# Softmax of 32 attention tiles: division moved into the transposing products, bias added by an identity product

## The chip, the cores and the metric

One NeuronCore of a Trainium2 chip runs the whole program. The metric is device time in microseconds (us), the median of the runs. The core has a matrix engine (PE, with its weight loads shown as PEld), a vector engine (DVE), a scalar engine (ACT), a general engine (POOL) and queues that issue transfers (SP above all). Each engine executes its own instructions in the order in which they stand; engines wait for each other by semaphores. PE reads both operands from SBUF and writes to PSUM banks of 128 x 512 f32.

## The reference: what is computed

Two layers on 256 latent tokens and 256 context tokens of width 1024. The first layer is attention and a dense feed-forward block, the second a pooling mixer and a mixture of eight experts. The change touches the attention's softmax alone:

```
s_loc = q . k * scale + bias         # neighbourhood heads: 8 heads, latent keys, bias and mask by head
s_ctx = q . k_ctx * scale            # the same heads, context keys, no bias
p = softmax(concat(s_loc, s_ctx))    # f32; the latent-attention heads (8 more) have no bias
out = p[:, :n_loc] @ v + p[:, n_loc:] @ v_ctx
```

All tensors are f32, and everything must come out to f32 accuracy.

## The kernel before

Attention works on 32 units. A unit is one head and 128 queries, so its scores are one PSUM bank of 128 queries x 512 keys. A block is a pair of heads with both query halves, four units. Blocks 4 to 7 (units 0 to 15) are the latent-attention heads, with scores from `QT` and `KT` (L605); blocks 0 to 3 (units 16 to 31) are the neighbourhood heads, with scores from `qaT` and `kaT` (L603) and a bias. There are three score banks, called `w`; the six products that build the bias table (L583) use them too.

For each unit `softmax` does: for neighbourhood units an add of the bias into the first 256 columns of the bank (DVE, L616); the negated row maximum (DVE, L618) and, for the latent units, its scaling (L621); exponential with row sums (ACT, L623) into an SBUF tile `sc`, of which there are four; reciprocal of the sums (DVE, L624); and the division of the 128 x 512 tile by a scalar for each row (DVE, L625). `turn` then transposes the tile in four 128 x 128 pieces on PE: L633 calls the helper whose line is L168, with the data as stationary and the identity as moving side, into a bank of `acc`; ACT copies that to `PT` (L633). When a block's four units are turned, `values` multiplies with the values (L641, bank `o`), ACT and DVE split the result in a high and a low part (L154, L155), and `project` multiplies these with a quarter of the output weights in three products each (L159 to L161).

The code runs over units: at every even unit i the scores of units i+4 and i+5 are issued, then unit i is turned, and values and projections follow by block. Three modulation jobs run alongside: eight DVE multiply-adds of 128 x 512 each (L316) and a few PE products (L345). POOL multiplies the output weights by the gate g1, four 128 x 2048 tiles (L650), and takes the low parts of the second half's weights (L155). The order on every engine but SP is set by a list scheduler at build time until the last unit is issued, so the code's order is a wish and not the order executed. After the attention the second half of the projection, the residual with its norm, and the feed-forward block follow on PE.

Of the kernel before, what the change touches and what calls it, by code (L numbers as in the profile page):

```python
# [7 lines left out]
F32 = mybir.dt.float32  # L8
# [3 lines left out]
OP = mybir.AluOpType  # L12
# [5 lines left out]
P = 128  # L18
D = 1024
KB = D // P  # L20
S = 256
# [81 lines left out]
class Trunk:  # L103
# [247 lines left out]
    def layer0_attention(self):  # L351
        tc, nc, I = self.tc, self.nc, self.I
# [3 lines left out]
        with ExitStack() as st:  # L356
            ent = lambda *a, **k: st.enter_context(tc.tile_pool(*a, **k))
            ap = ent(name="attn", bufs=1)
# [138 lines left out]
            qcT = ap.tile([P, 2, S], F32, name="qcT")  # L497
# [43 lines left out]
            qaT = ap.tile([P, 4, S], F32, name="qaT")  # L541
            kaT = ap.tile([P, 4, 512], F32, name="kaT")
            for j in range(4):
                t = self.ps()
# [10 lines left out]
            for j in range(4):  # L555
                t = self.ps()
# [12 lines left out]
            for rr in range(2):  # L569
                for h in range(8):  # L570
                    nc.sync.dma_start(brev[h // 4][rr * 64:rr * 64 + 64, (h % 4) * 384:(h % 4 + 1) * 384].rearrange("p (a b) -> p a b", a=6),
                                      bass.AP(tensor=rb.tensor, offset=rb.offset + h * 465 + (5 - rr) * 31 - 48,
                                              ap=[[1, 64], [31, 6], [1, 64]]))
# [3 lines left out]
            bias = ap.tile([P, 3200], F32, name="lw")[:, 0:3072].rearrange("p (h a b) -> p h a b", h=8, a=6)  # L577
# [12 lines left out]
            w_out = I["attn_w_out"][0].rearrange("(k p) f -> p k f", p=P)  # L590
            blocks = (4, 5, 6, 7, 0, 1, 2, 3)
            units = [(blk, u, qt) for blk in blocks for qt in range(2) for u in range(2)]
            scs, PTs, ws, wp = {}, {}, {}, {}

            def scores(i):

                s_ps = [self.ps() for _ in range(2)]
                for n in range(2):
                    blk, u, qt = units[i + n]
                    h = (blk % 4) * 2 + u  # L600
                    qs = slice(qt * P, (qt + 1) * P)
                    if blk < 4:
                        nc.tensor.matmul(s_ps[n], qaT[u * 64:u * 64 + 64, blk, qs], kaT[u * 64:u * 64 + 64, blk], start=True, stop=True)  # L603
                    else:
                        nc.tensor.matmul(s_ps[n], QT[:, h, qs], KT[:, h], start=True, stop=True)  # L605
                for n in range(2):
                    softmax(i + n, s_ps[n])

            def softmax(i, s_ps):
                blk, u, qt = units[i]  # L610
                h = (blk % 4) * 2 + u
                nmax = self.sm.tile([P, 1], F32, name="nmax", bufs=4)
                sc = tmp.tile([P, 512], F32, name="sc", bufs=4)
                scale = 1.0
                if blk < 4:
                    nc.vector.tensor_add(s_ps[:, 0:S], s_ps[:, 0:S],  # L616
                                         bias[:, h, 2 - 2 * qt:6 - 2 * qt].rearrange("p a b -> p (a b)"))
                nc.vector.reduce_max(nmax, s_ps, axis=AX.X, negate=True)  # L618
                if blk >= 4:
                    scale = MLA_SCALE  # L620
                    nc.vector.tensor_scalar(nmax, nmax, scale, None, op0=OP.mult)  # L621
                den = self.sm.tile([P, 1], F32, name="den", bufs=4)
                nc.scalar.activation(sc, s_ps, AF.Exp, bias=nmax, scale=scale, accum_out=den)  # L623
                nc.vector.reciprocal(den, den)  # L624
                nc.vector.tensor_scalar(sc, sc, den, None, op0=OP.mult)  # L625
                scs[i] = sc

            def turn(i):
                blk, u, qt = units[i]
                if (blk, u) not in PTs:  # L630
                    PTs[blk, u] = tmp.tile([P, 4, S], F32, name="PT", bufs=5)
                self.transposes(PTs[blk, u][:, :, qt * P:(qt + 1) * P], [scs[i][:, kt * P:(kt + 1) * P] for kt in range(4)],
                                lambda d, t: nc.scalar.copy(d, t.rearrange("p (k q) -> p k q", k=4)), self.acc)  # L633

            def values(blk):
                o_ps = self.ps("o")
# [30 lines left out]
            def meanwhile(k2):  # L667
                if k2 in (1, 2):
                    scores(2 * k2 - 2)
                if k2 > 1:  # L670
                    next_mod()
# [7 lines left out]
            for tt in range(4):  # L679
                t = self.acc()  # L680
# [5 lines left out]
            for i, (blk, u, qt) in enumerate(units):  # L686
                if i in (8, 16, 26):
                    self.mod_finish(int(i < 26), "o")
                    if mods:
                        self.mod_issue(*mods.pop(0))  # L690
                if i in (2, 4, 6, 8, 10, 12):
                    bias_block(i // 2 - 1)
                if i % 2 == 0 and i + 4 < len(units):
                    scores(i + 4)
                turn(i)
                if i % 4 == 0 and i:
                    values(units[i - 1][0])
                if i % 4 == 2:
                    if i > 4:
                        project(0, i // 4 - 1)  # L700
                    out_split(0, blk, w0[:, 2 * (i // 4 % 2):2 * (i // 4 % 2) + 2])
                if i == 16:
                    out_stream(1)
                if i == 19:

                    places = [ap.tile([P, 8, 512], F32R, name="t16"), ap.tile([P, 4, 512], F32R, name="o8"), e8k(0, F32R)]
                    later = [t[:, 2 * j:2 * j + 2] for t in places for j in range(t.shape[1] // 2)]
                if i > 20 and later:
                    out_split(1, blocks[8 - len(later)], later.pop(0), nc.gpsimd)
# [3 lines left out]
            for w in self.ffn_first[:2]:  # L713
                t = self.stream_slot().bitcast(F32R).rearrange("p (i k f) -> p i k f", i=2, k=KB)
# [11 lines left out]
            t = self.ps("o")  # L726
# [1009 lines left out]
```

## Time and profile before

| | |
|---|---|
| median of 3 runs | 1456.23 us (1454.86 to 1461.7) |
| profiled execution | 1459.44 us, span 1457.6 us |
| PE busy | 1360.4 us, 93% of the span |
| DVE, ACT, POOL busy | 725.8, 465.0, 105.4 us |
| mean granted TensorE clock | 0.97 |
| attention's units on PE | from 137 to about 237 us of the span |

PE's granted clock has two levels, 2.4 GHz (1.00 in the rows) and 1.2 GHz (0.50). A matmul's record includes the time until its last result is out, and the records of neighbours overlap; so the price of a product in a full stream is the distance between the starts, not the record's length. An f32 product is recorded as two matmuls; a row of the timeline merges neighbours of one kind and gives their count.

### The profile page before, as it was taken

To read this page: it belongs to the slowest core of one execution; us is meant where nothing else is said; L and a number is where in the kernel's file an instruction comes from. 1 tells how busy PE (TensorE), PEld (TensorE's weight loads), DVE (VectorE), ACT (ScalarE), POOL (GpSimd) and SP (SyncE) were. 2 spreads that over 40 slices of the span, in tenths; PEclk is the share of its full clock that TensorE was granted. 3 is DMA by queue.
4 is the path that set the end of the run, shared out by engine and by line. 5 is a ranking of instruction groups with operands and counts; after the bars stand their busy time and mean duration, and the time that the engine had idled before them with its cause. 6 is when DMAs were issued, how large, how long until landed. Compare 5 with 4: busy or idle time off the path is not lost. (4 is left out here: it accounts for less than half of the span.)

```text
span 1457.6 us, 22081 instructions
## 1 busy us (share of the span) xinstructions
PE 1360.4 (93%) x8817; PEld 841.2 (58%) x8817; DVE 725.8 (50%) x1156; ACT 465.0 (32%) x691; POOL 105.4 (7%) x66
## 2 busy tenths in 40 slices
PE   6898989799999999999999999999999999999995
PEld 4765546699998586555664333343333344667762
DVE  2769795587677765754572100011100015556653
ACT  3443462443442343544550000010000013345541
POOL 0344040301001100000000000000000000000000
PEclk9999989799999999999999999999999999999998
DMA  9775422699886669999999999999999999999994
GB/s 361 257 230 191 153 76 68 211 371 326 306 295 185 133 254 392 375 395 393 365 367 380 381 393 393 395 355 368 392 396 393 392 370 361 393 390 393 377 352 168
DMA packets 237561, 464.41 MB, mean 319 GB/s; under 512 B 31655, under 2 KB 76922, under 8 KB 237454
## 3 DMA queue, kind: packets, MB, share of 16 engines
q1 hardware_dynamic: 234582, 457.61, 87.1%
q10 hardware_dynamic: 2872, 5.33, 1.1%
q8 instruction: 71, 1.16, 0.3%
q14 instruction: 36, 0.29, 0.1%
HBM read 461.87 MB, written 1.05 MB: 318 GB/s over the span
## 5 line engine op out<-in xcount | busy, mean ns | idle before, releaser
L155 DVE TENSOR_TENSOR wh<-wt,wh 128x1024 fp32r<-128x1024 f32 (+1 forms) x243 | 291.9, 1217 | 78.8 <-ACT wh L154 71.9
L1649 PE MATMUL w<-wt,xg 128*32 128x256 f32 (+3 forms) x2496 | 314.3, 468 | 16.5 <-DMA wt<-in_moe_w_up_dram 16.5
L154 ACT CAST wh<-wt 128x1024 fp32r<-128x1024 f32 (+1 forms) x244 | 252.1, 1042 | 179.8 <-PE w L160 81.3
L1649 PEld LDWEIGHTS w<-wt,xg 128*32 128x32 f32 (+1 forms) x2496 | 120.7, 122 | 178.0 <-issue 125.5
L1709 PE MATMUL acc<-wt,aT 128*32 128x256 f32 (+2 forms) x1456 | 188.1, 464 | 0.0
L1656 DVE TENSOR_TENSOR a<-a,w 64x512 f32<-64x512 f32 (+4 forms) x58 | 31.2, 538 | 304.8 <-ACT a L1655 304.8
L1655 ACT ACTIVATE a<-w 64x512 f32<-64x512 f32 (+4 forms) x58 | 27.1, 467 | 427.9 <-PE w L1649 426.2
L1709 PEld LDWEIGHTS acc<-wt,aT 128*32 128x32 f32 (+2 forms) x1456 | 67.0, 120 | 105.8 <-issue 87.4
L316 DVE SCALAR_TENSOR_TENSOR raw<-wt,ccol,raw 128x512 f32<-128x512 f32 x105 | 101.2, 965 | 2.1
L161 PE MATMUL acc<-wh,aT 128*128 128x512 f32 x204 | 79.7, 391 | 0.0
L159 PE MATMUL w<-h2H,wh 128*128 128x256 f32 x272 | 77.2, 284 | 0.0
L161 PE MATMUL w<-h2H,wh 128*128 128x256 f32 x272 | 76.2, 280 | 0.0
L160 PE MATMUL w<-hT,wh 128*128 128x256 f32 x272 | 76.2, 280 | 0.0
L1620 POOL TENSOR_TENSOR wt<-wt,ln_g 128x256 f32<-128x256 f32 x1 | 1.0, 1013 | 954.0 <-ACT wt L1618 954.0
L160 PE MATMUL w<-wh,xgH 128*128 128x512 f32 (+1 forms) x144 | 56.6, 393 | 1.6 <-DVE wh L155 1.6
L159 PE MATMUL w<-wh,xgH 128*128 128x512 f32 (+1 forms) x144 | 56.8, 394 | 0.0
L161 PE MATMUL w<-wh,xgL 128*128 128x512 f32 (+1 forms) x144 | 55.7, 387 | 0.0
L160 PEld LDWEIGHTS w<-hT,wh 128*128 128x128 f32 x272 | 51.5, 189 | 0.6 <-issue 0.2
L161 PEld LDWEIGHTS w<-h2H,wh 128*128 128x128 f32 x272 | 51.6, 190 | 0.0
L159 PEld LDWEIGHTS w<-h2H,wh 128*128 128x128 f32 x272 | 51.1, 188 | 0.6 <-issue 0.2
L1649 PE MATMUL o<-wt,xg 128*32 128x256 f32 (+2 forms) x416 | 49.2, 459 | 0.0
L159 PE MATMUL acc<-wh,aH 128*128 128x512 f32 (+1 forms) x112 | 45.3, 404 | 0.0
(499 smaller groups left out, 2075.7 us busy)
## 6 DMA issues: line engine op xcount, KB each, us to landing
wt<-in_moe_w_down_dram SPq DMA_DIRECT2D x104, 1024.0 KB
wt<-in_moe_w_gate_dram SPq DMA_DIRECT2D x96, 1024.0 KB
wt<-in_moe_w_up_dram SPq DMA_DIRECT2D x96, 1024.0 KB
wt<-in_mod_w_dram SPq DMA_DIRECT2D x45, 1024.0 KB
wt<-in_moe_w_gate_dram SPq DMA_DIRECT2D x16, 896.0 KB
wt<-in_moe_w_up_dram SPq DMA_DIRECT2D x16, 896.0 KB
wt<-in_ffn_w_gate_dram SPq DMA_DIRECT2D x11, 1024.0 KB
wt<-in_ffn_w_up_dram SPq DMA_DIRECT2D x11, 1024.0 KB
```

The costliest lines, as they stand in the source:

```text
L154: nc.scalar.copy(hi, src)
L155: return (eng or nc.vector).tensor_sub(lo, src, hi.bitcast(F32))
L159: nc.tensor.matmul(out, lh, rh, start=start, stop=False, skip_group_check=True)
L160: nc.tensor.matmul(out, lh, rl, start=False, stop=False, skip_group_check=True)
L161: return nc.tensor.matmul(out, ll, rh, start=False, stop=stop, skip_group_check=True)
L316: nc.vector.scalar_tensor_tensor(acc, w[k], self.ccol[:, k:k + 1], mb if k == 0 else acc, op0=OP.mult, op1=OP.add)
L1620: eng.tensor_mul(o[:, cs], o[:, cs], g[:, hs][:, cs])
L1649: nc.tensor.matmul(t[b:b + M, 0:f1 - f0], xg[:, k], w[k][:, f0:f1], start=(k == 0), stop=(k == KB - 1), skip_group_check=True)
L1655: nc.scalar.activation(a[64:64 + r, f0:f1], t[0:r, f0:f1], AF.Silu)
L1656: nc.vector.tensor_mul(a[0:r, f0:f1], a[64:64 + r, f0:f1], t[64:64 + r, f0:f1])
L1709: nc.tensor.matmul(dacc[0][q2 * M:(q2 + 1) * M, 0:Dn], aT[0:bw, b, q * M:(q + 1) * M], wd[j][0:bw, q2 * Dn:(q2 + 1) * Dn], start=(first an ...
```

## The change

The division of the whole tile is gone. In its place DVE multiplies the 128 x 128 identity by the reciprocals, a scalar for each row, which gives a diagonal matrix (L639 of the changed kernel; four slots in one tile, named qcT like the tile whose memory it takes). The transposing products take this diagonal as moving side and are written as plain products (L642) instead of transposes. The DVE add of the bias is gone as well. PE adds it: after the scores of a neighbourhood pair, one product for each unit with the identity as stationary side and 256 columns of the bias table as moving side accumulates into the bank (L611). All else is as before.

```diff
--- before.py
+++ after.py
@@ -590,7 +590,8 @@
             w_out = I["attn_w_out"][0].rearrange("(k p) f -> p k f", p=P)
             blocks = (4, 5, 6, 7, 0, 1, 2, 3)
             units = [(blk, u, qt) for blk in blocks for qt in range(2) for u in range(2)]
-            scs, PTs, ws, wp = {}, {}, {}, {}
+            scs, dens, PTs, ws, wp = {}, {}, {}, {}, {}
+            dgs = ap.tile([P, 4, P], F32, name="qcT")
 
             def scores(i):
 
@@ -600,9 +601,16 @@
                     h = (blk % 4) * 2 + u
                     qs = slice(qt * P, (qt + 1) * P)
                     if blk < 4:
-                        nc.tensor.matmul(s_ps[n], qaT[u * 64:u * 64 + 64, blk, qs], kaT[u * 64:u * 64 + 64, blk], start=True, stop=True)
+                        nc.tensor.matmul(s_ps[n], qaT[u * 64:u * 64 + 64, blk, qs], kaT[u * 64:u * 64 + 64, blk], start=True, stop=False,
+                                         skip_group_check=True)
                     else:
                         nc.tensor.matmul(s_ps[n], QT[:, h, qs], KT[:, h], start=True, stop=True)
+                for n in range(2):
+                    blk, u, qt = units[i + n]
+                    if blk < 4:
+                        nc.tensor.matmul(s_ps[n][:, 0:S], self.ident,
+                                         bias[:, (blk % 4) * 2 + u, 2 - 2 * qt:6 - 2 * qt].rearrange("p a b -> p (a b)"),
+                                         start=False, stop=True, skip_group_check=True)
                 for n in range(2):
                     softmax(i + n, s_ps[n])
 
@@ -612,9 +620,6 @@
                 nmax = self.sm.tile([P, 1], F32, name="nmax", bufs=4)
                 sc = tmp.tile([P, 512], F32, name="sc", bufs=4)
                 scale = 1.0
-                if blk < 4:
-                    nc.vector.tensor_add(s_ps[:, 0:S], s_ps[:, 0:S],
-                                         bias[:, h, 2 - 2 * qt:6 - 2 * qt].rearrange("p a b -> p (a b)"))
                 nc.vector.reduce_max(nmax, s_ps, axis=AX.X, negate=True)
                 if blk >= 4:
                     scale = MLA_SCALE
@@ -622,15 +627,21 @@
                 den = self.sm.tile([P, 1], F32, name="den", bufs=4)
                 nc.scalar.activation(sc, s_ps, AF.Exp, bias=nmax, scale=scale, accum_out=den)
                 nc.vector.reciprocal(den, den)
-                nc.vector.tensor_scalar(sc, sc, den, None, op0=OP.mult)
+                dens[i] = den
                 scs[i] = sc
 
             def turn(i):
                 blk, u, qt = units[i]
                 if (blk, u) not in PTs:
                     PTs[blk, u] = tmp.tile([P, 4, S], F32, name="PT", bufs=5)
-                self.transposes(PTs[blk, u][:, :, qt * P:(qt + 1) * P], [scs[i][:, kt * P:(kt + 1) * P] for kt in range(4)],
-                                lambda d, t: nc.scalar.copy(d, t.rearrange("p (k q) -> p k q", k=4)), self.acc)
+
+                dg = dgs[:, i % 4]
+                nc.vector.tensor_scalar(dg, self.ident, dens[i], None, op0=OP.mult)
+                t = self.acc()
+                for kt in range(4):
+                    nc.tensor.matmul(t[:, kt * P:(kt + 1) * P], scs[i][:, kt * P:(kt + 1) * P], dg, start=True, stop=True,
+                                     skip_group_check=True)
+                nc.scalar.copy(PTs[blk, u][:, :, qt * P:(qt + 1) * P], t.rearrange("p (k q) -> p k q", k=4))
 
             def values(blk):
                 o_ps = self.ps("o")
```

On PE, neighbourhood units 20 to 24 and their surroundings, first before, then changed (L603 and L604 are scores, L168 and L642 a unit's turn, L641 and L652 values, L159 to L161 the projection):

```order
L603 MATMUL w<-kaT,qaT 128x512 x2
L168 MATMUL acc<-cst,sc 128x128 x4
L641 MATMUL o<-PT,e_1114 64x256 x8
L168 MATMUL acc<-cst,sc 128x128 x4
L603 MATMUL w<-kaT,qaT 128x512 x2
L168 MATMUL acc<-cst,sc 128x128 x4
```

```order
L604 MATMUL w<-kaT,qaT 128x512 x2
L611 MATMUL w<-lw,cst 128x256 x2
L642 MATMUL acc<-qcT,sc 128x128 x4
L652 MATMUL o<-PT,e_1111 64x256 x8
L642 MATMUL acc<-qcT,sc 128x128 x4
L604 MATMUL w<-kaT,qaT 128x512 x2
L611 MATMUL w<-lw,cst 128x256 x2
```

The place of scores, turns and values is the same; each pair of scores is followed at once by its two bias products, so that the first unit's maximum stands behind the second unit's score as well.

On DVE, the first neighbourhood units, again before and then changed (L618 and L623 are the maxima, L155 the low part of a block's values or of weights):

```order
L624 RECIPROCAL den<-den 128x1
L616 TENSOR_TENSOR w<-w,lw 128x256
L625 TENSOR_SCALAR sc<-sc,den 128x512
L618 TENSOR_REDUCE nmax<-w 128x1
L616 TENSOR_TENSOR w<-w,lw 128x256
L155 TENSOR_TENSOR e_1116<-o,e_1115 128x256
L618 TENSOR_REDUCE nmax<-w 128x1
```

```order
L639 TENSOR_SCALAR qcT<-cst,den 128x128
L623 TENSOR_REDUCE nmax<-w 128x1 x2
L629 RECIPROCAL den<-den 128x1
L639 TENSOR_SCALAR qcT<-cst,den 128x128
L155 TENSOR_TENSOR e_1113<-o,e_1112 128x256
```

The 128 x 512 divisions and the adds have left the row; a 128 x 128 multiply stands where a division stood. The orders of POOL and SP are the same in both kernels.

## Rows read from the trace of the kernel before

**Rows 1.** Busy table by stretch: PE, PEld, DVE, ACT, POOL; granted clock, DMA share, GB/s.
```profile
146.70:153.00 6.30, 6.28 (x14) 3.59 (x15) 3.37 (x9) 3.05 (x7) 0.00 (x0) 0.53 0.25 97
153.00:181.20 28.20, 28.20 (x139) 15.58 (x137) 23.89 (x55) 14.08 (x34) 2.31 (x1) 1.00 0.46 153
181.20:192.00 10.80, 6.91 (x27) 4.78 (x28) 10.54 (x12) 4.84 (x11) 8.04 (x4) 0.68 0.27 88
192.00:211.00 19.00, 15.48 (x69) 7.82 (x68) 19.00 (x35) 12.67 (x27) 10.95 (x7) 0.82 0.32 111
211.00:236.60 25.60, 24.57 (x140) 14.72 (x141) 16.61 (x42) 14.38 (x33) 1.28 (x4) 1.00 0.00 1
```

**Rows 2.** Timeline of PE: start, length, line, count (waits in brackets); latent units.
```profile
161.52 0.47 PE L159 MATMUL acc<-e,e 128*128 128x512 f32 x1
...
162.99 0.60 PE L168 MATMUL acc<-cst,sc 128*128 128x128 f32 x4
163.43 0.95 PE L345 MATMUL o<-ones,raw 128*128 128x1 f32 x8
164.24 1.10 PE L583 MATMUL w<-wt,cst 128*128 128x512 f32 x2
...
167.43 1.95 PE L641 MATMUL o<-PT,e 128*64 128x256 f32 x16
169.31 0.66 PE L168 MATMUL acc<-cst,sc 128*128 128x128 f32 x4
```

**Rows 3.** Timeline of PE, neighbourhood units.
```profile
185.14 2.07 PE L603 MATMUL w<-kaT,qaT 64*128 64x512 f32 x2 [3.89 <-ACT sc L623]
...
191.76 1.13 PE L603 MATMUL w<-kaT,qaT 64*128 64x512 f32 x4
192.82 0.65 PE L168 MATMUL acc<-cst,sc 128*128 128x128 f32 x4
```

**Rows 4.** A line's instructions: count, duration min/median/max, first and last start.
```profile
L168 PE MATMUL acc<-cst,sc x128: 270/273/477, 137.2 to 233.2; 128*128 128x128 f32 x128
...
L1489 PE MATMUL acc<-cst,sl x16: 272/275/359, 531.9 to 537.4; 128*128 128x128 f32 x16
```

**Rows 5.** Timeline of PE, later layer: eight plain products L1489, twice four.
```profile
531.95 1.06 PE L1489 MATMUL acc<-cst,sl 128*128 128x128 f32 x8
532.90 1.10 PE L1347 MATMUL o<-sl,xn 128*128 128x64 f32 x8
...
536.52 1.19 PE L1489 MATMUL acc<-cst,sl 128*128 128x128 f32 x8
537.65 0.65 PE L1649 MATMUL o<-wt,xg 128*64 128x512 f32 x2
```

**Rows 6.** Timeline of PE, later layer: a plain product with 256 moving columns.
```profile
482.30 0.59 PE L1036 MATMUL w<-A,xn 128*128 128x256 f32 x2
482.73 0.40 PE L1037 MATMUL w<-A,xn 128*128 128x136 f32 x2
```

**Rows 7.** Groups by line: count, busy us, mean ns, idle before.
```profile
L625 DVE TENSOR_SCALAR sc<-sc,den 128x512 f32<-128x512 f32 x32 | 25.0, 780 | 0.4
L618 DVE TENSOR_REDUCE nmax<-w 128x1 f32<-128x512 f32 x32 | 21.6, 680 | 12.1 <-PE w L605 12.1
L616 DVE TENSOR_TENSOR w<-w,lw 128x256 f32<-128x256 f32 x16 | 6.6, 422 | 2.9 <-PE w L603 2.9
...
L623 ACT ACTIVATE sc<-w,nmax 128x512 f32<-128x512 f32 x32 | 22.0, 689 | 22.8 <-DVE nmax L621 14.9 <-DVE nmax L618 6.1 <-PE w L603 1.6
...
L465 DVE TENSOR_SCALAR lw<-lw,rsy 128x128 f32<-128x128 f32 x4 | 1.0, 281 | 0.0
```

**Rows 8.** Timeline of DVE and of POOL, around the first neighbourhood scores.
```profile
178.98 4.70 DVE L625 TENSOR_SCALAR sc<-sc,den 128x512 f32<-128x512 f32 x1
...
178.89 4.51 POOL L650 TENSOR_TENSOR wt<-wt,g 128x2048 f32<-128x2048 f32 x1 [35.64 <-DMA wt<-in_attn_w_out_dram]
```

**Rows 9.** Timeline of SP's queue: the first transfers issued behind the attention.
```profile
249.46 0.92 SPq L128 DMA_DIRECT2D wt<-in_mod_w_dram  x2
```

## The prediction, made before the changed kernel had run

> **What bounds the kernel now.** I read the page first (PE busy nearly throughout), then the busy table cut at the attention's stages, then the timelines of PE and DVE in it. The change touches 137 to 237 us alone; there the reader is to see two regimes [rows 1]. From 146.7 to 181.2 us PE is busy without a gap: the latent units, and PE is the bound (the first 6 us at the lower clock, 0.53, after an idle stretch). DVE is busy 27.3 of these 34.5 us, so it is not. From 181.2 to 211 us it is the other way: DVE is busy 29.5 of 29.8 us, PE only 22.4, and PE's granted clock falls to 0.68 and 0.82. From 211 to 236.6 us PE is again busy 24.6 of 25.6 us at full clock.
>
> So the same edit, which takes work from DVE and gives work to PE, costs time in the first and third stretch and can give some back in the second. Behind the attention the shift goes through one to one: no transfer is under way from 211 to 236.6 us (1 GB/s, [rows 1]), and the next ones are issued at 249.46 us [rows 9], so no stream has run ahead that would swallow a delay or withhold a gain.
>
> **What each part costs.**
> The turn. Before, four transposes a unit: 128 records for 32 units [rows 4], so one record each, and four of them take 0.44 us of a full stream (162.99 to 163.43, [rows 2]). The changed kernel writes them as plain f32 products with the same 128 x 128 shapes. The trace has this very form, stationary data and the identity as moving side, in a later layer: L1489, eight products in the code and 16 records [rows 4], so two records each; four products (x8) take 0.95 us from start to start (531.95 to 532.90), and in a second place 1.13 us [rows 5]. The cheap bound is two records at the transposes' rate, 0.88 us. I take 0.95, the row in a full stream: +0.51 us a unit on PE. That is the change's main price, and the diff does not show it: the number of products is the same.
>
> The Trainium skill's page "TensorE: Matmul & The Clock Gate", section Terms, says that the transpose mode is four times faster for FP32. The rows say 2.2 times (0.95 by 0.44). By the page's factor the turn would cost 1.76 us; no row here shows that.
>
> The bias. Sixteen products with 256 moving columns. The nearest row is L1036, the same shape: two records, 0.43 us from start to start [rows 6]. Bounds: 0 if they fill waits, 0.59 if each is exposed to the end of its record. I take 0.43 where PE is the bound: 0.87 us a pair.
>
> Scores. Two neighbourhood scores side by side run together on the two halves of the rows: four records in 1.06 us [rows 3]. After the change they always stand as pairs, with the bias products behind.
>
> DVE. 32 divisions go, 25.0 us with the stalls in them, and 16 adds, 6.6 us; 32 multiplies of 128 x 128 come, at 0.28 us (L465, the same form) 9.0 us [rows 7]. So DVE is about 22 us lighter, if no new multiply is held up. Alone this gains nothing; it counts where DVE is the bound.
>
> The hold-ups. In the two stretches where POOL multiplies a 128 x 2048 tile, one division of 0.48 us takes 4.70 and the other 4.66 us, from POOL's start to its end ([rows 8], the first of the two). The bias add and the maximum, which read PSUM, show no such thing. The new multiply has the division's kind (TENSOR_SCALAR, SBUF to SBUF), so it can be held up just as long; POOL's order is unchanged. The Trainium skill's page "SBUF — State Buffer", section "SBUF: two separate sides", gives the reason: DVE and GpSimd share a pair of ports that one of them holds for a whole instruction. By that rule the shorter multiply is no cure, and the trace agrees. What changes is how long PE can go on meanwhile.
>
> **The sum, by PE's stream.**
> 146.7 to 181.2 us. 12 units are turned here: 12 x 0.51 = 6.1. In the new order the bias products of units 16 to 19 stand in it, 4 x 0.43 = 1.7. PE has no gap to hide them: +7.8 us.
>
> 181.2 to 236.6 us, 55.4 us long. PE's work in it after the change, at full clock: 6 pairs of scores with bias, 6 x (1.06 + 0.87) = 11.6; 18 turns, 17.1; 5 values at 1.88 (167.43 to 169.31, [rows 2]), 9.4; 5 projections of 1.47 (161.52 to 162.99), 7.4; 3 modulation sums of 0.81, 2.4. Together 47.9 us. The same list with the prices before is about 34 us, so some 21 us of this stretch were waits, lower clock and scores that ran singly, and they can hide the added 14. The 1.0 us in which PE is idle after 211 us [rows 1] I leave in, for the chain of the last unit. Without any other wait the stretch would be 48.9 us.
>
> The waits that stay: PE needs a score bank, which the exponential two pairs back frees. Between a pair's bias products and the next pair lie two turns and a projection or values, 1.9 + 1.5 = 3.4 us or more; the chain behind a score, maximum 0.68 and exponential 0.69 [rows 7], is 1.4. That leaves a lead of 2 us. Each of the two hold-ups costs DVE 4.2 us, so about 2 us of PE each: 4. For a backlog of DVE around the modulation job I put 1 us more. 53.9 us, -1.5 against before.
>
> Stalls before 146.7 us: PE waited there for a maximum behind DVE's multiply-adds that POOL held up; four shorter scalings ahead of it give DVE some 0.8 us, but POOL's second tile still ends when it ended. Bounds: -1 to 0; I take 0.
>
> Sum: 7.8 - 1.5 = +6.3 us. The profiled execution's 1459.44 us (a span of 1457.6 and 1.8 around it) would become 1465.7. It was 3.2 us above the median of the runs, 1456.23, so I put the median at 1462.5, or 1463 us. What a measurement of this kernel can tell from no change is about 0.5%, 7.3 us: the forecast lies just at its edge.
>
> **The rivals.**
> 1. Slower still: the hold-ups cost PE as much as before. In front of the score at 185.14 PE idled 3.89 us [rows 3], and between 181.2 and 211 us the idle sum is 3.9 + 3.5 = 7.4 us; by the clocks 0.68 and 0.82 about 6.9 us each were at the lower level, which cost 3.5 and some 3 us [rows 1]. If these 13.9 us stay instead of 5, the second stretch is 62.8 us and the sum 7.8 + 7.4 = +15.2: 1471. For it: same kind of DVE instruction, same POOL work, and a first unit whose maximum now waits for both scores and both bias products. Against it: PE takes 2.7 us a unit instead of about 2, and DVE has fewer instructions queued behind the one held up. It decides if PE waits more than about 3 us for a bank or a diagonal.
> 2. No change: PE never waits, and the turn costs the cheap bound, 0.88. First stretch 12 x 0.44 + 1.7 = 7.0, second 47.9 - 1.3 + 1.0 = 47.6, -7.8; sum -0.8: 1455. For it: DVE is 22 us lighter. Against it: the two hold-ups.
> 3. Faster: the product with a diagonal is executed like a transpose, one record of 0.11 us. Then the first stretch gains only 1.7 and the second is 47.9 - 9.2 + 1.0 = 39.7, -15.7 us: 1442. For it: same shapes and the same number of products. Against it: L1489 has exactly this form and two records each.
> 4. Each plain product passes through the array four times at the transposes' 0.11 us, 1.76 us a turn: first stretch 12 x 1.32 + 1.7 = 17.5, second 47.9 + 18 x 0.81 + 1.0 = 63.5, +8.1; sum +25.6: 1482. That is what the factor on the page would do. The rows of L1489 speak against it.
>
> **How the numbers follow.** Forecast 0.47 (1458 to 1468 as its own range), rival 1 0.28, rival 2 0.17, rival 3 0.04, rival 4 0.04. L1489's dearer place (1.13) would add 30 x 0.18 = 5.4 us to the forecast and is within the range. Slower by over 0.5% (above 1463.5) are rivals 1 and 4 and somewhat less than half of the forecast's case: 0.50. Faster by over 0.5% (below 1449) is rival 3 and a little for what I don't see: 0.07. Within 0.5%: 0.43. The range leaves out rivals 3 and 4 and the far end of rival 1: 1454 to 1473.
>
> **What will show it.** Right: L642 has 256 records, and eight of them take about 0.95 us from start to start; L611 has 32 records, 0.43 us a product; the latent units' stretch is about 8 us longer with PE still without a gap; between the first neighbourhood scores and the last projection PE has the full clock nearly throughout, with one or two waits of some 2 us where a DVE multiply of the diagonal takes over 4 us beside POOL. Wrong: 128 records of L642 (rival 3); a granted clock of 0.5 for several us after a wait in the neighbourhood units (rival 1); no long multiply and no wait at all (rival 2); or a stretch behind the attention, such as the feed-forward block, whose length has changed by more than 1 us.

## The result and the profile after

| | before | changed |
|---|---|---|
| median of 6 runs each | 1458.55 us (1454.86 to 1465.73) | 1472.69 us (1468.18 to 1474.7) |
| ratio, 95% interval | | 1.0088 [1.0065, 1.011] |
| profiled execution, span, mean clock | 1459.44, 1457.6 us, 0.970 | 1472.8, 1470.8 us, 0.971 |

The change costs 14.1 us. The forecast was 1463 us, 6.8 us above the 1456.23 us known then, with a range of 1454 to 1473. The sign was right, but the change is twice as large as forecast. The time is 9.7 us above the forecast; 2.3 of these are the six runs of before, whose median is that much higher than that of the first three. That it still lies inside the range, by 0.3 us, is luck.

The shift arises in the attention and stays. From PE's first scores after the stall to the first product of the last projection (L159 with a wait of 0.46 us ahead of it in both kernels) before took 146.72 to 236.60, 89.9 us, and the changed kernel takes 146.67 to 250.24, 103.6 us. From there to the end of the span it is 1221.0 us before and 1220.6 us after. So +13.7 us in the stage and nothing behind it.

First the busy line of the page after, then the rows of three lines: count, duration min/median/max in ns, first and last start.

```profile
PE 1383.1 (94%) x8977; PEld 868.8 (59%) x8977; DVE 708.9 (48%) x1140; ACT 465.0 (32%) x691; POOL 104.0 (7%) x66
```

```profile
L642 PE MATMUL acc<-qcT,sc x256: 270/275/421, 137.3 to 246.9; 128*128 128x128 f32 x128
L611 PE MATMUL w<-lw,cst x32: 379/379/774, 180.7 to 234.0; 128*128 128x256 f32 x32
L639 DVE TENSOR_SCALAR qcT<-cst,den x32: 267/286/1990, 115.9 to 240.7; 128x128 f32<-128x128 f32 x32
```

The turn has 256 records where [rows 4] had 128, so two a product, and the bias products bring 32. The multiplies of the diagonal take 0.29 us in the median; the longest took 1.99 us. No instruction of DVE is held up for 4.7 us as in [rows 8].

The busy table cut at the places that answer to [rows 1] (busy us of PE, PEld, DVE, ACT, POOL; then granted clock, DMA share, GB/s):

```profile
146.67:153.00 6.33, 6.33 (x18) 4.21 (x19) 3.05 (x9) 2.34 (x7) 0.00 (x0) 0.51 0.00 0
153.00:188.70 35.70, 35.70 (x195) 23.23 (x194) 22.39 (x59) 17.11 (x41) 7.16 (x3) 1.00 0.44 148
188.70:211.00 22.30, 20.37 (x108) 13.74 (x108) 20.20 (x31) 13.66 (x31) 13.50 (x8) 1.00 0.30 95
211.00:231.00 20.00, 20.00 (x116) 13.90 (x114) 9.44 (x27) 9.19 (x22) 0.00 (x0) 0.92 0.00 1
231.00:250.20 19.20, 18.68 (x105) 14.63 (x104) 3.56 (x9) 6.12 (x13) 0.81 (x4) 0.82 0.00 1
```

Up to 188.7 us PE works through the same twelve turns and three values as before up to 181.2, without a gap (and one more score, with four bias products). Behind it PE idles only 2.5 us, against 8.4 before [rows 1], and still the second part is longer than before: 61.5 us (188.75 to 250.24) against 55.4. So most of the growth is PE's own work, which grew or ran slower. DVE is busy less than half of the time from 211 us on, but not ahead of that: from 195 to 210 us it is busy 14.9 of 15.0 us, and there lie the two waits that will matter below:

```profile
200.00:205.00 5.00, 4.00 (x17) 2.28 (x17) 5.00 (x9) 3.72 (x9) 1.84 (x2) 1.00 0.51 148
205.00:210.00 5.00, 4.07 (x18) 2.38 (x16) 4.89 (x10) 3.52 (x6) 1.44 (x1) 1.00 0.18 74
```

The timeline of PE (start, length, line, count, waits in brackets), the latent units; it answers to [rows 2]:

```profile
162.33 1.06 PE L642 MATMUL acc<-qcT,sc 128*128 128x128 f32 x8
163.14 0.48 PE L159 MATMUL acc<-e,e 128*128 128x512 f32 x1
...
164.61 1.05 PE L642 MATMUL acc<-qcT,sc 128*128 128x128 f32 x8
165.50 0.95 PE L345 MATMUL o<-ones,raw 128*128 128x1 f32 x8
```

A turn takes 0.81 us from start to start in front of a projection, where it took 0.36 (161.16 to 161.52 of before), and 0.89 us in front of a modulation sum, where it took 0.44. The neighbourhood units, which answer to [rows 3]:

```profile
185.64 2.21 PE L604 MATMUL w<-kaT,qaT 64*128 64x512 f32 x4
187.78 1.13 PE L611 MATMUL w<-lw,cst 128*128 128x256 f32 x4
188.75 1.05 PE L642 MATMUL acc<-qcT,sc 128*128 128x128 f32 x8
...
192.80 2.10 PE L604 MATMUL w<-kaT,qaT 64*128 64x512 f32 x4
194.82 1.13 PE L611 MATMUL w<-lw,cst 128*128 128x256 f32 x4
...
199.74 1.12 PE L604 MATMUL w<-kaT,qaT 64*128 64x512 f32 x2
201.87 1.12 PE L604 MATMUL w<-kaT,qaT 64*128 64x512 f32 x2 [1.00 <-ACT sc L628]
202.92 1.13 PE L611 MATMUL w<-lw,cst 128*128 128x256 f32 x4
...
207.15 1.12 PE L604 MATMUL w<-kaT,qaT 64*128 64x512 f32 x2
209.20 1.12 PE L604 MATMUL w<-kaT,qaT 64*128 64x512 f32 x2 [0.93 <-ACT sc L628]
210.25 1.42 PE L611 MATMUL w<-lw,cst 128*128 128x256 f32 x4
...
228.04 1.12 PE L604 MATMUL w<-kaT,qaT 64*128 64x512 f32 x2
229.09 1.05 PE L345 MATMUL o<-ones,raw 128*128 128x1 f32 x8
230.08 1.12 PE L604 MATMUL w<-kaT,qaT 64*128 64x512 f32 x2
231.13 1.61 PE L345 MATMUL o<-ones,raw 128*128 128x1 f32 x8
232.60 2.05 PE L611 MATMUL w<-lw,cst 128*128 128x256 f32 x4
234.45 1.91 PE L642 MATMUL acc<-qcT,sc 128*128 128x128 f32 x8
...
250.24 0.50 PE L159 MATMUL acc<-e,e 128*128 128x512 f32 x1 [0.46 <-ACT e L154]
```

A pair of scores that runs side by side takes 1.06 us. Here five of eight pairs didn't: 2.14 us from the first score to the bias products at 185.64, 2.02 at 192.80, 3.18 and 3.10 with a wait inside, and at 228.04 two single scores of 1.05. A score stands on half of the rows, and the second of a pair can only run beside the first if its bank is free at that time. A row that reads "x4, 2.10" is a split pair without a visible gap: PE counts as busy for twice the time. The pair at 228.04 is another case: no bank was late there, for the order itself puts the products of one column (L345) between its scores, so the bias products don't follow this pair at once, as they do the others. Single scores are not new either. Before, 8 of the 16 neighbourhood scores ran singly, some by the order (214.04, 216.19 and 218.83 us) and some behind a late bank:

```profile
196.71 1.12 PE L603 MATMUL w<-kaT,qaT 64*128 64x512 f32 x2
198.26 1.12 PE L603 MATMUL w<-kaT,qaT 64*128 64x512 f32 x2 [0.42 <-ACT sc L623]
```

In the changed kernel, from 231.1 to 238.5 us every row is about twice as long: the granted clock is at the lower level, with no idle time of PE ahead of it.

Why the second bank was late at the first of these pairs, the timeline of ACT and of POOL shows:

```profile
185.38 0.62 ACT L154 CAST t<-wt 128x512 fp32r<-128x512 f32 x1 [5.29 <-POOL wt L661]
185.91 0.68 ACT L628 ACTIVATE sc<-w,nmax 128x512 f32<-128x512 f32 x1
...
180.81 4.53 POOL L661 TENSOR_TENSOR wt<-wt,g 128x2048 f32<-128x2048 f32 x1 [37.04 <-DMA wt<-in_attn_w_out_dram]
...
187.30 4.57 POOL L661 TENSOR_TENSOR wt<-wt,g 128x2048 f32<-128x2048 f32 x1
```

ACT executes in order. A cast of the weights that POOL is scaling waits 5.29 us for POOL's tile, and the exponential that frees a score bank stands behind it. DVE, meanwhile, has no multiply to be held up with. At POOL's second tile it has one: it starts at 189.97 and ends at 191.96, when that tile has ended; this is the 1.99 us above.

At the two dearest pairs, 199.74 and 207.15, the timelines point to DVE and its modulation job. No run leaves that job out, so this is read and not tested. The second score at 201.87 waits for the exponential at 201.03, and that one waited 5.16 us for its row maximum, which stood on DVE behind multiply-adds of that job, two of them of about 1.7 us (0.74 us elsewhere):

```profile
196.10 1.68 DVE L316 SCALAR_TENSOR_TENSOR raw<-wt,ccol,mbz 128x512 f32<-128x512 f32 x1
...
197.82 1.65 DVE L316 SCALAR_TENSOR_TENSOR raw<-wt,ccol,raw 128x512 f32<-128x512 f32 x1
...
200.24 0.68 DVE L623 TENSOR_REDUCE nmax<-w 128x1 f32<-128x512 f32 x1
...
201.03 0.69 ACT L628 ACTIVATE sc<-w,nmax 128x512 f32<-128x512 f32 x1 [5.16 <-DVE nmax L623]
```

From the end of the bias products at 195.79 to the end of this exponential, 201.72, are 5.9 us. For the next pair it is 5.2 us (203.89 to 209.05): the maximum came at 207.58, behind the same job, and two casts on ACT until 208.46.

### The profile page after: what moved, and what is told of

The parts are those of the page before. It is cut to its first block, busy times and chain, and to the rows that moved or that the text cites. A ratio compares the mean times of both kernels' runs of the same rounds, so it can differ in the third digit from the quotient of the medians.

```text
span 1470.8 us, 22417 instructions
## 1 busy us (share of the span) xinstructions
PE 1383.1 (94%) x8977; PEld 868.8 (59%) x8977; DVE 708.9 (48%) x1140; ACT 465.0 (32%) x691; POOL 104.0 (7%) x66
## 3 DMA queue, kind: packets, MB, share of 16 engines
q10 hardware_dynamic: 2872, 5.33, 1.0%
HBM read 461.87 MB, written 1.05 MB: 315 GB/s over the span
## 5 line engine op out<-in xcount | busy, mean ns | idle before, releaser
L155 DVE TENSOR_TENSOR wh<-wt,wh 128x1024 fp32r<-128x1024 f32 (+1 forms) x243 | 296.3, 1235 | 79.9 <-ACT wh L154 72.3
L316 DVE SCALAR_TENSOR_TENSOR raw<-wt,ccol,raw 128x512 f32<-128x512 f32 x105 | 93.5, 890 | 2.2
L161 PE MATMUL acc<-wh,aT 128*128 128x512 f32 x204 | 79.7, 391 | 0.0
L159 PE MATMUL w<-h2H,wh 128*128 128x256 f32 x272 | 77.3, 284 | 0.0
L161 PE MATMUL w<-h2H,wh 128*128 128x256 f32 x272 | 76.3, 280 | 0.0
L159 PE MATMUL w<-wh,xgH 128*128 128x512 f32 (+1 forms) x144 | 56.8, 394 | 0.0
L161 PE MATMUL w<-wh,xgL 128*128 128x512 f32 (+1 forms) x144 | 55.8, 388 | 0.0
L161 PEld LDWEIGHTS w<-h2H,wh 128*128 128x128 f32 x272 | 51.6, 190 | 0.0
L159 PEld LDWEIGHTS w<-h2H,wh 128*128 128x128 f32 x272 | 51.1, 188 | 0.6 <-issue 0.2
L159 PE MATMUL acc<-wh,aH 128*128 128x512 f32 (+1 forms) x112 | 45.3, 405 | 0.0
```

Of the source, the lines that this page charges most:

```text
L155: return (eng or nc.vector).tensor_sub(lo, src, hi.bitcast(F32))
L159: nc.tensor.matmul(out, lh, rh, start=start, stop=False, skip_group_check=True)
L161: return nc.tensor.matmul(out, ll, rh, start=False, stop=stop, skip_group_check=True)
L316: nc.vector.scalar_tensor_tensor(acc, w[k], self.ccol[:, k:k + 1], mb if k == 0 else acc, op0=OP.mult, op1=OP.add)
```

## The experiments

Medians and ratios against the kernel before on the same chip. The profiled stage is the stretch defined above, from the first scores after the stall to the last projection's first product.

**The division alone** (the changed kernel with the bias add back on DVE).

```diff
-                        nc.tensor.matmul(s_ps[n][:, 0:S], self.ident, bias[...], start=False, stop=True, ...)
+                if blk < 4:
+                    nc.vector.tensor_add(s_ps[:, 0:S], s_ps[:, 0:S], bias[...])
```

> The division by plain products with the diagonal alone; the bias is added by DVE as before. Theory A (the price is PE's: two records for each plain product where a transpose has one): 32 turns at about 0.47 us more on PE, all of it shown in the latent units' stretch (146.7 to 181.2 us of before becomes some 5.5 us longer), about half of it hidden in the neighbourhood units: +7 to +10 us in all. Theory B (the price is the bias product and what it does to the pair of scores): at most +6 us, nothing beyond the latent units. Theory C (rival 1: DVE held up beside POOL): the granted clock falls to 0.5 after waits of PE for a diagonal, +10 us or more.

Measured: 1465.92 us (1463.1 to 1469.13), ratio 1.0051 [1.0037, 1.0066], stage 97.1 us. It is 7.2 us by the medians, as theory A had it. More than half of the loss is the division's.

**The bias alone** (the kernel before, with the identity product for the bias).

```diff
+                        nc.tensor.matmul(s_ps[n][:, 0:S], self.ident, bias[...], start=False, stop=True, ...)
-                    nc.vector.tensor_add(s_ps[:, 0:S], s_ps[:, 0:S], bias[...])
```

> The bias by identity products alone; DVE divides the tile and PE transposes as before. Theory A: PE gets 16 products of 0.43 us, 6.9 us, in a stretch of the neighbourhood units that had some 21 us of slack, and DVE loses 6.6 us there: -1 to +4 us. Theory B (a first unit's maximum waits for both scores and both bias products, and second scores run singly behind a late bank): +6 us or more.

Measured: 1459.99 us, ratio 1.0008 [0.9993, 1.0024]: no change that can be told in the whole. In the attention there is one: the profiled stage took 93.9 us and ended 5.4 us later than before's (242.03). The stretch behind it was 5.1 us shorter than before's (1215.9 us for 1221.0). Most of that lies in the expert layer, whose first products came 4.6 us later (542.2 for 537.6 us) and whose last came 0.8 us later (1434.4 for 1433.6); why, is open.

By the medians the two parts add to +0.59%, and together they cost +0.88%, some 4 us more, though the intervals leave room for less. By the ends of the profiled stages they add up without a rest: 8.3 us later with the division alone, 5.4 with the bias alone, 13.6 with both.

**The second record without DVE's relief** (the kernel before, division on DVE as it was, the turn as plain products with the identity).

```diff
-                self.transposes(PTs[blk, u][...], [scs[i][...] for kt in range(4)], ...)
+                    nc.tensor.matmul(t[:, kt * P:(kt + 1) * P], scs[i][...], self.ident, start=True, stop=True, ...)
```

> The kernel before with one edit: a turn's four transposes are written as plain products with the identity as moving side, the form of L1489. Division and bias stay on DVE. Theory A: 256 records in place of 128, 0.47 us a turn; the latent units' stretch 5.5 us longer, and as DVE is not relieved, more of the rest is exposed than with the diagonal: +8 to +13 us. If the number of records is not the price: within 2 us of before.

Measured: 1472.51 us, ratio 1.0087 [1.0062, 1.0113], stage 100.2 us. The timeline of PE in it:

```profile
160.14 1.05 PE L634 MATMUL acc<-cst,sc 128*128 128x128 f32 x8
161.12 1.95 PE L644 MATMUL o<-PT,e 128*64 128x256 f32 x16
```

Two records a product with the identity as well, 0.98 us a turn here. It is the plain product that costs, not the diagonal. Against the division alone the diagonal's relief of DVE is worth 1.0087 less 1.0051, 0.36% or about 5 us by the medians; the intervals touch.

**The bias ahead of the scores** (the changed kernel; the bias product opens the accumulation, the scores follow as a pair).

```diff
-                        nc.tensor.matmul(s_ps[n], qaT[...], kaT[...], start=True, stop=False, ...)
-                        nc.tensor.matmul(s_ps[n][:, 0:S], self.ident, bias[...], start=False, stop=True, ...)
+                        nc.tensor.matmul(s_ps[n][:, 0:S], self.ident, bias[...], start=True, stop=False, ...)
+                        nc.tensor.matmul(s_ps[n], qaT[...], kaT[...], start=False, stop=True, ...)
```

> The changed kernel with the bias products issued ahead of their pair of scores, so that the wait for the second bank falls on a bias product and the two scores follow each other at once. Theory D (5 of 8 pairs of scores ran singly in the changed kernel, which cost some 6 us): all pairs in about 1.06 us, 4 to 6 us shorter than the changed kernel, +8 to +10 us against before. Rival (the scores ran singly because a bank came late, and PE waits for it wherever the wait is put): within 2 us of the changed kernel.

Measured: 1468.46 us, ratio 1.0067 [1.0046, 1.0087], stage 98.2 us. The timeline of PE:

```profile
188.19 0.70 PE L602 MATMUL w<-lw,cst 128*128 128x256 f32 x2 [0.79 <-ACT sc L628]
188.81 1.13 PE L610 MATMUL w<-kaT,qaT 64*128 64x512 f32 x4
```

The wait for the second bank now falls on the second bias product, and both scores run behind it side by side: all eight pairs took 1.06 to 1.16 us from start to start. At the first two late banks this gains nothing, as the rival had it: a pair with its bias products took 3.07 and 2.97 us, wait included, for 3.11 and 2.99 in the changed kernel. The second part, up to 246.25 us, is 5.1 us shorter all the same (56.4 us for 61.5). PE idled more in it, 4.0 us for 2.5; what it gained is pairs side by side and the clock, which was full from 215 us to the stage's end and cost 1.7 us in all (0.89 and 0.77 from 205 to 215 us) instead of 5.2.

**POOL's multiply in pieces** (the changed kernel; the 128 x 2048 gate multiply as four of 128 x 512).

```diff
-                    nc.gpsimd.tensor_mul(w, w, g1[:, None, hs].to_broadcast([P, 4, 512]))
+                    for k in range(4):
+                        nc.gpsimd.tensor_mul(w[:, k], w[:, k], g1[:, hs])
```

> The changed kernel with POOL's multiplication of the output weights by g1 cut into four instructions of 128 x 512 each. Theory E (second scores ran singly and late in the changed kernel because ACT stood 5.3 us behind a cast that waited for POOL's whole tile, and DVE beside it): the first cast is released after some 1.2 us, the scores from 185 to 210 us run as pairs, PE idles less; 3 to 6 us shorter than the changed kernel, +8 to +11 against before. Rival (the exponentials are late by the chain of each unit itself): within 2 us of the changed kernel.

Measured: 1465.66 us (1457.29 to 1472.84), ratio 1.0061 [1.0036, 1.0086]. Its end of the stage is 243.83 us where the changed kernel had 250.24. Of these 6.4 us, 4.5 lie ahead of the stage, which began at 142.21; the stage itself took 101.6 us for 103.6. Two of the three pairs between 185 and 210 us ran side by side, much as theory E had it, but PE now waited 2.63 us for a cast of ACT at 187.09. By its interval alone the gain over the changed kernel isn't certain, and neither is the one of the experiment ahead of it. Hence the two together:

**Both** (the bias ahead, and the pieces).

> The changed kernel with both cures together: the bias products ahead of the scores (a pair's four score records then stand side by side) and POOL's gate multiply in four pieces of 128x512. Each alone gave about 4.2 us (ratio 1.0067) and about 6 us (1.0061) against the changed kernel. Theory F (two separate losses: scores that ran singly with the lower clock behind them, and ACT and DVE behind POOL's long tile): the gains add, about 10 us, 1461 to 1463 us, ratio 1.002 to 1.004; all eight neighbourhood pairs of scores at about 1.1 us, the stage from the first scores after the stall to the last projection's first product at 91 to 94 us, no lower granted clock between 215 and 245 us. Rival G (one and the same loss: ACT's late exponential makes the bank late, and that is what splits the pairs, so either cure takes it all): 1466 to 1468 us, ratio 1.006, stage 97 us. What neither cure touches is the turn's second record, 32 x 0.4 to 0.5 us = 13 to 16 us on PE less what DVE's relief hides; so neither theory lets it come below the kernel before with the same pieces, 1451.78 us.

Measured: 1462.04 us (1457.39 to 1469.21), ratio 1.0026 [1.0004, 1.0048]; this interval and that of the changed kernel lie apart. 0.62% of the 0.88% are gone, about 9 us. The total is as the theory of two separate losses had it; the profiled stage, 98.6 us (144.92 to 243.50) for 91 to 94, is not: it began 1.75 us earlier and ended 6.7 us earlier than the changed kernel's, and one wait of PE (2.86 us for ACT's cast at 191.32) took back a part, with a clock of 0.89 from 185 to 200 us.

**The pieces in the kernel before** (same edit).

> The kernel before with POOL's multiplication cut into the same four instructions. Theory E: the two divisions of 4.7 us become at most 1.7 us, PE's waits of 3.89 and 2.57 us and the lower clock behind them shrink or go: -4 to -10 us. Rival (POOL's total is the same and DVE meets it four times as often): within 2 us of before.

Measured: 1451.78 us (1448.86 to 1457.73), ratio 0.9968 [0.9948, 0.9988]: faster than both kernels. The stage began 4.5 us earlier (142.23) and took 85.4 us for 89.9, so half of the gain in the profile arises ahead of it. The waits in it didn't all go: PE still idled 3.67 us in front of the score at 189.43, for an exponential that had waited 5.02 us for its maximum on DVE. The division's row, and POOL's two stretches beside the attention, which answer to [rows 8]:

```profile
L625 DVE TENSOR_SCALAR sc<-sc,den x32: 473/482/1542, 115.8 to 222.1; 128x512 f32<-128x512 f32 x32
...
173.25 5.33 POOL L651 TENSOR_TENSOR wt<-wt,g 128x512 f32<-128x512 f32 x4 [27.57 <-DMA wt<-in_attn_w_out_dram]
...
179.96 6.04 POOL L651 TENSOR_TENSOR wt<-wt,g 128x512 f32<-128x512 f32 x4
```

POOL takes longer in all (5.33 and 6.04 us for a tile instead of 4.51 and 4.56), and a division is held up for at most 1.54 us, about one piece, instead of 4.70. That is the rule of the Trainium skill's page "SBUF — State Buffer", section "SBUF: two separate sides", by which one of the two engines holds the shared ports for a whole instruction; the trace agrees, and here a shorter instruction on the other engine shortened the hold-up.

**The bias ahead, transposes and division as before, and pieces** (an attempt at something still faster).

> No diagonal: DVE divides and PE transposes as before; the bias is added by identity products issued ahead of the pair of scores, and POOL's multiplication is in four pieces. Theory A with D and E: the turns cost nothing more, the scores run as pairs, 6.9 us of PE work are added in the neighbourhood units and 6.6 us of DVE work go: -6 to 0 us against before, and within 3 us of the kernel before with pieces alone. Theory B: slower than that one by 4 us or more.

Measured: 1455.32 us, ratio 0.9985 [0.9969, 1.0002]: not better than the pieces by themselves. Taking the add from DVE shows no gain, with the pieces or without them.

**One record a product** (the changed kernel with the turn as transposes; the diagonal is still made but not used, so this kernel leaves the division out of its result).

```diff
-                    nc.tensor.matmul(t[:, kt * P:(kt + 1) * P], scs[i][...], dg, start=True, stop=True, ...)
+                self.transposes(PTs[blk, u][...], [scs[i][...] for kt in range(4)], ...)
```

> The changed kernel with the turn as transposes by the identity again: the diagonal is still made on DVE but not used, so the division is left out of the result. All else (no DVE division, bias as an identity product on PE) stays. It measures what the second record costs in the changed kernel's own setting. Theory H (the second record is the whole loss, and it costs PE's stream 0.4 to 0.5 us for each of 32 turns, 13 to 16 us): 1457 to 1460 us, ratio 0.998 to 1.001, L168 with 128 records and 0.44 us a turn. Rival I (with PE lighter, its other waits come back: the same bank and the same exponential end the same pairs): 6 to 8 us of the 13 to 16 are kept, 1464 to 1467 us, ratio 1.004 to 1.006. Rival J, the prediction's own arithmetic for one record (its third rival): 1442 us, ratio 0.990.

Measured: 1454.93 us (1451.8 to 1459.47), ratio 0.9977 [0.996, 0.9994].

```profile
L168 PE MATMUL acc<-cst,sc x128: 270/273/421, 139.5 to 235.0; 128*128 128x128 f32 x128
```

The stage took 89.6 us (148.77 to 238.38), as before's 89.9 and 14.0 less than the changed kernel's. By the medians the second record is 1.0088 less 0.9977, 1.11% or about 16 us (0.7 to 1.5% by the ends of the intervals): as much as the whole loss, which is theory H, though the time is 2 us below its range. What the change gives without it is -0.23%, some 3 us. It is not the only way to get time back: "both" took 9 us from the loss with the second record in place, so the prices of the parts don't simply add.

## Why the forecast had the sign and missed the size

**The turn's second record: right.** It was read from a later layer's plain product, +0.51 us a turn. Measured, by what follows the turn, are +0.45 (0.81 for 0.36 us, 0.89 for 0.44) to +0.51 (1.00 for 0.49). That the diff hides the price (the same number of products) and that the identity would cost as much as the diagonal, two experiments showed.

**First part, +7.8 us: right, in part by luck.** From the first scores to the end of the bias products of the second neighbourhood pair it was 42.1 us (146.67 to 188.75) for 34.5, so +7.6. The twelve turns gave the 6.1 us as forecast: ten at the full clock 0.47 us more each, two at the lower clock 0.68 each. The split pair at 185.64 took 1.1 us more and the bias products 0.2. Against that, about 1.6 us went where values and other products no longer stand in two pieces. The forecast had neither.

**Second part, -1.5 us: wrong.** It came out +6.1. The list of PE's work was complete: 18 turns, six pairs, five values, five projections, three sums, 47.9 us as priced. The step that failed is the one on the scores and their banks, in two places. "After the change they always stand as pairs, with the bias products behind", at 1.06 us: one pair doesn't stand so in the order (228.04), and the others don't run as pairs when the second bank is late. And the chain behind a score, put at 1.4 us with a lead of 2 and with 1 us for a backlog of DVE around the modulation job, took 5.9 and 5.2 us beside that job.

In the second part the split pairs cost, beyond 1.06 us each, 0.96 (at 192.80), 2.12 (199.74), 2.04 (207.15) and 1.04 us (228.04), 6.2 together, of which 1.9 are visible as waits; 4.2 of them are the two pairs behind the modulation job. The lower clock, for which the forecast had nothing, took 5.2 us: the granted clock was 0.66 from 210 to 215 us, 0.64 from 230 to 235 and 0.67 from 235 to 240, and one less the clock, times 5 us each, is the work not done (1.7 + 1.8 + 1.7). With 2.5 us of idle PE that makes 47.9 + 4.3 + 5.2 + 2.5 = 59.9 of 61.5 us; 1.6 are spread over small rows, dearer bias products among them (0.97 us a pair for 0.87).

Put the other way: of the 55.4 us before, the forecast took some 21 for waits, lower clock and single scores, and let 14 us of new work vanish in them. PE's idle time did fall, from 8.4 to 2.5 us. The lower clock went from some 6.5 us only to 5.2, and the single scores stayed.

**The hold-ups: the right cause in the wrong place.** 4 us of waits were charged to diagonal multiplies of over 4 us. The longest took 1.99 us. Beside POOL's first tile DVE had no such instruction to execute; ACT stood 5.29 us behind the same tile instead, in a cast, with the exponential behind it. The loss showed as a split pair, not as idle PE. That cutting the tile helps is shown for the kernel before by its time (0.9968) and, together with the bias ahead, for the changed one; by which waits, only in part.

**The rivals.** "Slower still", by waits and a lower clock in the second part, came nearest (1471 us by its price, nearer than the forecast). One of its signs showed, a lower clock for several us in the neighbourhood units. The other did not: it asked for waits of more than about 3 us for a bank or a diagonal, and the longest for a bank was 1.00. So its time is right in part by luck. "No change" and "one record" fell with 256 records. The factor of four on the Trainium skill's page "TensorE: Matmul & The Clock Gate", section Terms, fell too: 0.89 by 0.44 us, in the same place, is about 2.

**Behind the attention: right for this change.** The shift stayed to within 0.4 us. It needn't: with the bias alone and with the bias ahead of the scores, 5.1 and some 6 us of the shift were gone at the end of the profiled execution.

## What to carry to other kernels

Here an f32 transpose is one record and a plain f32 product of the same shape two, so an arithmetic step folded into a transposing product doubled that product; count records, not products, in the form that it will have. Half-height products that are to run side by side need both their banks at that moment: putting what must wait for a bank ahead of both made all pairs run together, though at two of the late banks the wait was as long as the gain. Look at what stands in the queue ahead of the instruction that frees a bank: a cast that waits for POOL on ACT (5.29 us), a job's multiply-adds on DVE (a maximum late by over 4 us). And a long POOL instruction holds up DVE (a division of 0.48 us took 4.70) and, through the data it makes, ACT; cutting it in four made the kernel before 0.3% faster, which neither part of the change did.

## What the runs showed of the hardware beyond that

The granted clock fell at 231 us while PE had been busy without a gap for over 20 us. What stood ahead of it were single half-height scores in turn with products of one column. The same sequence (L604, L345, L604, L345, L611) stands in three kernels with the fall: the changed one, the bias alone (at 225.8) and the pieces in the changed kernel (at about 225). In the one-record kernel it stands too, and the clock stayed full:

```profile
221.72 1.12 PE L604 MATMUL w<-kaT,qaT 64*128 64x512 f32 x2
222.77 1.05 PE L345 MATMUL o<-ones,raw 128*128 128x1 f32 x8
223.75 1.12 PE L604 MATMUL w<-kaT,qaT 64*128 64x512 f32 x2
224.81 1.05 PE L345 MATMUL o<-ones,raw 128*128 128x1 f32 x8
225.72 1.11 PE L611 MATMUL w<-lw,cst 128*128 128x256 f32 x4
```

There the second L345 ran into the next product at full clock. With other neighbours the two single scores stand between such products in four more kernels: the clock fell to 0.50 in the identity's plain products (236 to 238 us) and in the bias ahead with pieces and transposes (224 to 226), and stayed full in the division alone and in the pieces in the kernel before. Where this pair ran side by side (the changed kernel with the bias ahead, with and without pieces) there was no fall in this place. So the sequence goes with the fall but doesn't decide it, and what does is open.
